# The second column group's planes split and sent one weight pair later in the up projection of a hybrid encoder layer

## The chip, the cores and the metric

The kernel runs on one core of one Trainium2 chip, as one launch. The metric is the device time of that launch in microseconds (us). The kernel before was timed three times: 1333.12, 1335.69 and 1338.51 us, median 1335.69 us.

## The reference, cut to what matters

One encoder layer on 256 tokens of width 2048, in float32: an input projection, two attention branches, a gated merge and output projection, and then an MLP of width 8192. The change lies in the MLP's first half, whose result goes on to the second half:

```python
h = rms_norm(x, norm_mlp_pre[l])
u = jnp.square(jax.nn.relu(jnp.einsum('bsd,df->bsf', h, w_up[l])))      # 256 x 8192
x = x + rms_norm(jnp.einsum('bsf,fd->bsd', u, w_down[l]), norm_mlp_post[l])
```

## The kernel before

**Numbers in two planes.** Every float32 operand of a product is split into a high plane (a cast to `F32R`, on ACT) and a low plane (the operand less the high plane, on DVE). A product is three matmuls: high by high, high by low, low by high.

**The up projection.** `w_up` (2048 x 8192) is worked off in eight groups `g` of 1024 columns, each a call of `wide_group` (L826). A group walks through eight weight pairs: pair `i` is the 256 rows from 256 `i` of the group's 1024 columns, in the order of `UPS` (L1253): 1, 2, 0, 4, 3, 6, 5, 7. Position `n` in this list is what the code counts, so n = 1 is pair 2, n = 2 pair 0, n = 3 pair 4, n = 4 pair 3. Six pairs are multiplied plainly (24 matmuls of 128x512 each); pairs 0 and 3 go by seven block products instead of eight (21 matmuls each), so a group has 186 matmuls. Results gather in eight PSUM banks; the plain pairs write banks 1, 2, 3 and 7, the seven products all but bank 7.

**One weight pair** (`pair_weights`, L696): a 1 MB load on SP's queue (L700) into one of three raw buffers; the high plane (L710, or L715 for pairs 0 and 3) on ACT into one of three buffers; the low plane (L712 or L719) on DVE into one of three. Pairs 0 and 3 also need sums of weight blocks on DVE (L716 to L718, tiles `t`), with planes of their own (`eh` on ACT, L728; `el` on DVE, L729). `Weights.next` (L750) writes the loads and splits of up to three pairs ahead into the program before the pair that is now multiplied.

**The end of a group.** After pair 3 the seven products are combined on ACT and DVE (`combine`, L820 to L824). After the last pair, 7, each of the four plain banks is added (`u_piece`, L1250, on DVE) and passed through ReLU (L1251, on ACT). The first L1250 reads bank 1, which is the bank that the next group writes first.

**What a group's result goes through during the next group** (`up_each`, L1287). A group's 1024 columns are two column groups `c` of 512. For the down projection they have to be transposed. For groups 1 to 6 this is done by DMA: `sent` (L732) splits 512 columns of both token halves into their upper and lower 16 bits (two ACT copies, L736) and issues one transposing DMA on SP's queue (L738); `joined` (L741) puts the 16-bit halves together again (one ACT copy, L743). The square follows (L1307), and `u_sets` (L1241) with `act_sets` (L1168) makes sums for the first column group (four on DVE, L1176 to L1179, tile `sm`), high planes (`ah`, L1191, ACT) and low planes (`al`, L1192, DVE), which go out to DRAM (L1195, on GpSimd's queue). The code before calls `sent` for both column groups at n = 1, `joined` for the first at n = 3 and for the second at n = 5. Group 7 transposes on TensorE.

**The down projection** reloads those planes by DMAs issued from ACT (`act_again`, L1200, L1208; tiles `bh`, `bl`).

**What sets the order.** Each engine and each DMA queue works off its instructions in the order in which they stand. That order is not the order of the Python code: the program is built with a scheduler (`schedule_with_timeline_sim`, at the top of the file) that places the instructions on each engine by its own estimate of when they can run. A call that is moved in the code thus also moves instructions that the code does not name. Temporary tiles (`page`) take their buffers from one ring of 27 in the order of the code.

## Time and profile before

| | |
|---|---|
| median of three runs | 1335.69 us |
| the profiled execution's own time | 1333.76 us |
| its span, first to last instruction | 1332.0 us |
| mean granted TensorE clock | 0.997 |
| ACT / DVE / TensorE busy | 816.1 / 1075.1 / 1319.7 us |
| up projection, groups 1 to 7 | about 687 to 988 us of the span |

Rows of a timeline give the start (us from the span's start), the duration, engine, line and operation, output and inputs by the program's names without buffer numbers, the shape, the count, and in brackets how long the engine idled before it and what released it. In the up projection three kinds of tile are called `u`: the PSUM banks, a group's result, and the transposed column groups; weight planes are `u_1h` (pair 1, high), `u_1l` (low), `u_3eh`, `u_3el`, `u_3t`, and `u_1r` is the raw load. `SPq` and `ACTq` are the DMA issues of SP and ACT. Matmuls are pipelined: one starts while the one before it is still draining.

### The profile page before, as it was taken

How to read it: one execution, taken by the hardware profiler on the slowest of the kernel's cores; microseconds unless marked ns; L12 is line 12 of the kernel's file. 1: busy time of each engine (PE TensorE's matmuls, PEld its weight loads, DVE VectorE, ACT ScalarE, POOL GpSimd, SP SyncE). 2: the span in 40 equal slices, each digit the busy share in tenths (PEclk: the TensorE clock that was granted, in tenths of full speed). 3: DMA queues.
4: the chain of work that ended last, by engine and by line, in shares of the span. 5: the costliest groups of instructions: out<-in, count | busy, mean ns of one | idle time of the engine just before them, and what ended most of it. 6: DMA issues, size and time to landing. Idle time of an engine off the chain costs nothing.

```text
span 1332.0 us, 16065 instructions
## 1 busy us (share of the span) xinstructions
PE 1319.7 (99%) x6163; PEld 1100.9 (83%) x6163; DVE 1075.1 (81%) x1245; ACT 816.1 (61%) x909; POOL 39.2 (3%) x73
## 2 busy tenths in 40 slices
PE   9999999999999999999999999999999999999997
PEld 8888888888888888888888888888888788888886
DVE  7968866777778879885678788888878888898886
ACT  6657584754554665554477788788755555555542
POOL 0000000000000000000100000000100000000000
PEclk9999999999999999999999999999999999999999
DMA  9885766665565667567658888888897998698895
GB/s 347 276 227 173 226 190 187 208 184 169 178 221 190 208 203 252 190 212 265 219 195 274 288 281 286 310 291 278 290 357 289 391 358 332 236 383 330 349 360 201
DMA packets 155917, 346.33 MB, mean 260 GB/s; under 512 B 58560, under 2 KB 59072, under 8 KB 155840
## 3 DMA queue, kind: packets, MB, share of 16 engines
q1 hardware_dynamic: 136160, 276.36, 61.6%
q10 hardware_dynamic: 12960, 43.26, 8.5%
q0 software_dynamic: 6720, 25.69, 4.7%
q8 instruction: 48, 0.79, 0.2%
q14 instruction: 29, 0.24, 0.0%
HBM read 307.01 MB, written 29.61 MB: 253 GB/s over the span
## 4 chain that ended last, share of the span: by engine, by line
PE 68%; issue 23%; DVE 4%; ACT 3%; DMA 2%; POOL 0%; SPq 0%; POOLq 0%; ACTq 0%; DVEq 0%
PE u L793 19%; PE ga L793 6%; PE gb L793 6%; PE ba L793 3%; PE bb L793 3%; PE y L793 3%; PE qn_p L224 2%; PE ka_p L224 2%; PE kn_p L224 2%; PE qa_p L224 2%; PE p L793 1%; PE qn_p L226 1%; PE ka_p L226 1%; PE vn_p L267 1%; PE vn_p L268 1%
## 5 line engine op out<-in xcount | busy, mean ns | idle before, releaser
L224 PE MATMUL qn_p<-hT,qn_h 128*128 128x512 f32 x128 | 45.5, 398 | 0.0
L793 PE MATMUL u<-u_1h,h2T 128*128 128x512 f32 x128 | 43.8, 393 | 1.5 <-DVE u L1250 1.3
L224 PE MATMUL ka_p<-hT,ka_h 128*128 128x512 f32 x128 | 45.0, 396 | 0.0
L224 PE MATMUL kn_p<-hT,kn_h 128*128 128x512 f32 x128 | 44.9, 397 | 0.0
L224 PE MATMUL qa_p<-hT,qa_h 128*128 128x512 f32 x128 | 44.2, 405 | 0.1
L793 PE MATMUL u<-u_2h,h2T 128*128 128x512 f32 x128 | 43.2, 391 | 0.0
L793 PE MATMUL u<-u_5h,h2T 128*128 128x512 f32 x128 | 41.9, 389 | 0.0
L793 PE MATMUL u<-u_6h,h2T 128*128 128x512 f32 x128 | 41.8, 389 | 0.0
L793 PE MATMUL u<-u_4h,h2T 128*128 128x512 f32 x128 | 41.5, 391 | 0.0
L793 PE MATMUL u<-u_7h,h2T 128*128 128x512 f32 x128 | 40.7, 389 | 0.0
L226 PE MATMUL qn_p<-hT,qn_l 128*128 128x256 f32 x128 | 35.9, 281 | 0.0
L226 PE MATMUL kn_p<-hT,kn_l 128*128 128x256 f32 x128 | 35.5, 280 | 0.0
L226 PE MATMUL ka_p<-hT,ka_l 128*128 128x256 f32 x128 | 34.9, 281 | 0.0
L226 PE MATMUL qa_p<-hT,qa_l 128*128 128x256 f32 x128 | 32.5, 282 | 0.1
L793 PEld LDWEIGHTS u<-u_1h,h2T 128*128 128x128 f32 x128 | 24.0, 188 | 8.3 <-ACT u L1307 3.4
L743 ACT COPY u<-u_g 128x2048 uint16<-128x2048 uint16 x12 | 30.3, 2527 | 0.0
L224 PEld LDWEIGHTS qn_p<-hT,qn_h 128*128 128x128 f32 x128 | 24.1, 188 | 5.6
L146 DVE TENSOR_TENSOR y_l<-y_w,y_h 128x1024 fp32r<-128x1024 f32 x16 | 19.0, 1222 | 11.9 <-ACT y_h L138 11.9
L712 DVE TENSOR_TENSOR u_4l<-u_4r,u_4h 128x2048 fp32r<-128x2048 f32 x8 | 18.3, 2293 | 12.5 <-ACT u_4h L710 12.5
L712 DVE TENSOR_TENSOR u_7l<-u_7r,u_7h 128x2048 fp32r<-128x2048 f32 x8 | 18.3, 2293 | 12.5 <-ACT u_7h L710 12.5
L224 PEld LDWEIGHTS kn_p<-hT,kn_h 128*128 128x128 f32 x128 | 23.8, 188 | 5.5
L224 PEld LDWEIGHTS qa_p<-hT,qa_h 128*128 128x128 f32 x128 | 24.0, 192 | 5.1 <-ACT qa_h L144 0.3
(1624 smaller groups left out, 4568.3 us busy)
## 6 DMA issues: line engine op xcount, KB each, us to landing
bh<-keeph ACTq DMA_DIRECT2D x30, 512.0 KB, 9.2
bl<-keepl ACTq DMA_DIRECT2D x30, 512.0 KB, 11.1
keeph<-ah POOLq DMA_DIRECT2D x18, 512.0 KB, 4.8
keepl<-al POOLq DMA_DIRECT2D x18, 512.0 KB, 4.7
va_w<-in_w_in SPq DMA_DIRECT2D x8, 1024.0 KB, 5.5
qn_w<-in_w_in SPq DMA_DIRECT2D x8, 1024.0 KB, 5.2
kn_w<-in_w_in SPq DMA_DIRECT2D x8, 1024.0 KB, 5.1
vn_w<-in_w_in SPq DMA_DIRECT2D x8, 1024.0 KB, 5.1
```

Source lines behind the costliest of these rows:

```text
L146: sub = nc.vector.tensor_sub(lo[part], src, hi[part].bitcast(F32)).ins
L224: nc.tensor.matmul(ps[b], hi[:, k % 4, cs], mv, start=(k == 0), stop=False)
L226: nc.tensor.matmul(ps[b][:, :T], lo[:, k % 4, cs], mv[:, :T], start=False, stop=(k == nk - 1))
L267: nc.tensor.matmul(ps[t], sh, hi[:, k % 4], start=(k == 0), stop=False)
L268: nc.tensor.matmul(ps[t], sh, lo[:, k % 4], start=False, stop=False)
L712: nc.vector.tensor_sub(l1, raw, h1.bitcast(F32))
L743: nc.scalar.copy(dst.rearrange("p k q -> p (k q)") .bitcast(U16) .rearrange("p (k t q h) -> p t h k q", k=4, t=2, h=2), got.rearrange("p ( ...
L793: ins = nc.tensor.matmul(self.ps[i], st, mv[:, blk], start=i not in self.begun, stop=last and n == 2).ins
```

## The change

One number. In `up_each` the second column group's `sent` call moves from n = 1 to n = 2, that is behind the loads and splits of pair 3 in the code; the first one's stays.

```diff
                 if by_dma and c in (0, 1):
-                    if n == (1, 1)[c]:
+                    if n == (1,2)[c]:
                         uh[cg] = sent([uz[t][:, c] for t in range(2)], f"u{cg}")
                     if n == (3,5)[c]:
                         us[cg] = page([P, 4, T], F32, f"u{cg}")
                         joined(uh[cg], us[cg])
```

What the scheduler makes of it is shown at three places of group 5; the groups 2 to 6 read alike. First ACT, in the middle of the group. `u9_s` are the split planes of the second column group of group 4 (number 9 of 16), `u8` the first one's transposed tile, `u5_3eh` the high planes of the sums of pair 3.

```order
 L710 CAST u5_6h_7380<-u5_6r_7378 128x2048
-L736 COPY u9_s_7305<-u40_7131 128x1024
-L736 COPY u9_s_7305<-u41_7132 128x1024
-L728 CAST u5_3eh0_7345<-u5_3t0_7338 128x1024
+L728 CAST u5_3eh0_7340<-u5_3t0_7333 128x1024
+L728 CAST u5_3eh1_7344<-u5_3t1_7334 128x1024
 L710 CAST u5_5h_7436<-u5_5r_7434 128x2048
-L728 CAST u5_3eh1_7349<-u5_3t1_7339 128x1024
+L736 COPY u9_s_7348<-u40_7131 128x1024
+L736 COPY u9_s_7348<-u41_7132 128x1024
+L710 CAST u5_7h_7470<-u5_7r_7468 128x2048
 L743 COPY u8_7384<-u8_g_7303 128x2x2x4x128
```

The two copies stand behind the cast of pair 5 instead of ahead of the sums' casts; the cast of pair 7 now stands ahead of the first column group's L743 instead of behind it. Further on, the cast of the next group's pair 1 stands ahead of the cast of `sm`'s planes instead of behind it. On DVE the sums of pair 3 (L716, L717) likewise stand ahead of, not behind, the low planes of pairs 3 and 6.

Second DVE, at the end of group 5 and the start of group 6. `u50` and `u51` are the result's two token halves as outputs, and as last inputs also banks of group 5; `al81` is the low plane of the column group's sums.

```order
+L712 TENSOR_TENSOR u6_1l_7512<-u6_1r_7509,u6_1h_7511 128x2048
 L1192 TENSOR_TENSOR al81_7403<-sm8_7387,ah81_7402 128x1024
-L712 TENSOR_TENSOR u6_1l_7512<-u6_1r_7509,u6_1h_7511 128x2048
 L821 TENSOR_TENSOR u50_7461<-u50_7461,u55_7371 128x512
-L712 TENSOR_TENSOR u6_2l_7542<-u6_2r_7539,u6_2h_7541 128x2048
 L822 TENSOR_TENSOR u51_7462<-u50_7461,u56_7367 128x512
 L1250 TENSOR_TENSOR u50_7461<-u50_7461,u51_7266 128x512
 L823 TENSOR_TENSOR u50_7461<-u54_7363,u50_7461 128x512
 L824 TENSOR_TENSOR u51_7462<-u54_7363,u51_7462 128x512
+L712 TENSOR_TENSOR u6_2l_7542<-u6_2r_7539,u6_2h_7541 128x2048
```

The low plane of the next group's pair 1 has moved ahead of `al81`, and that of pair 2 has moved from between L821 and L822 to behind L824, and so behind the first L1250. At the start of group 2 the order was this already in the kernel before.

Third PE, where pair 6 of group 5 ends. Before:

```order
L793 MATMUL u53_7280<-u5_6h_7380,h2T6_5190 128x512
L793 MATMUL u52_7273<-u5_5h_7436,h2T5_5189 128x512
L793 MATMUL u53_7280<-u5_5h_7436,h2T5_5189 128x512
L793 MATMUL u53_7280<-u5_5l_7437,h2T5_5189 128x512
L793 MATMUL u53_7280<-u5_5h_7436,h2T5_5189 128x512 x2
```

And now:

```order
L793 MATMUL u57_7287<-u5_6h_7380,h2T6_5190 128x512
L793 MATMUL u51_7266<-u5_5h_7436,h2T5_5189 128x512
L793 MATMUL u51_7266<-u5_5l_7437,h2T5_5189 128x512
L793 MATMUL u51_7266<-u5_5h_7436,h2T5_5189 128x512 x2
L793 MATMUL u51_7266<-u5_5l_7437,h2T5_5189 128x512
```

Before, pair 6's last matmul stood behind the first 12 of pair 5 (all of bank 51, most of bank 52); now all 24 of pair 5 stand behind it, because pair 3's matmuls moved ahead into the middle of pair 6. On SP's queue the second transposing DMA moves from behind the load of pair 5 to behind those of pair 7 and of the next group's pair 1, so the load of the next pair 2 stands directly behind it. In group 1 the order in the middle differs a little more, and at its end the cast of the next pair 2 moves behind the second column group's L743, L1307 and L1191. In group 7 and at the start of the down projection some casts and low planes change places with their neighbours; there ACT's DMA issues of the reloads (L1208) move ahead of one cast each.

## The prediction

> **What bounds the kernel now.** I read the page's busy line first, for the engine that could set the end.

> ```profile
> PE 1319.7 (99%) x6163; PEld 1100.9 (83%) x6163; DVE 1075.1 (81%) x1245; ACT 816.1 (61%) x909; POOL 39.2 (3%) x73
> ```

> TensorE is busy for 1319.7 of 1332.0 us. Next come the windows cut at two groups of the up projection (columns: length, then busy time and count of PE, PEld, DVE, ACT, POOL; granted clock, DMA share, GB/s).

> ```profile
> 815.50:858.20 42.70, 42.44 (x186) 34.83 (x187) 36.26 (x35) 34.40 (x30) 3.23 (x6) 1.00 0.89 293
> 858.20:900.80 42.60, 42.40 (x186) 34.81 (x186) 36.20 (x35) 34.56 (x30) 3.23 (x6) 1.00 0.85 288
> ```

> One group is 186 matmuls, and DVE (36.2 us) and ACT (34.5 us) have some 6 and 8 us of room in it. So a moved ACT copy costs something only if it makes TensorE wait. TensorE's own waits over the whole span are few:

> ```profile
> PE p L793 <- DMA bl<-keepl: 1.5, 1, 1.5
> PE u L793 <- DVE u L1250: 1.3, 4, 0.5
> PE u L793 <- ACT u L1307: 0.2, 1, 0.2
> ```

> The two rows of `u` are the five starts of groups 3 to 7; the first is one wait in the down projection. How much such a start really costs is read from the starts of the matmuls in the timeline of PE. Here are the first matmul of groups 2 to 7, and around the start of group 6 its neighbours.

> ```profile
> 730.07 0.39 PE L793 MATMUL u<-u_1h,h2T 128*128 128x512 f32 x1
> 772.58 0.47 PE L793 MATMUL u<-u_1h,h2T 128*128 128x512 f32 x1 [0.18 <-ACT u L1307]
> 815.51 0.47 PE L793 MATMUL u<-u_1h,h2T 128*128 128x512 f32 x1 [0.49 <-DVE u L1250]
> 858.21 0.47 PE L793 MATMUL u<-u_1h,h2T 128*128 128x512 f32 x1 [0.26 <-DVE u L1250]
> 900.22 0.39 PE L793 MATMUL u<-u_7h,h2T 128*128 128x512 f32 x1
> 900.87 0.47 PE L793 MATMUL u<-u_1h,h2T 128*128 128x512 f32 x1 [0.26 <-DVE u L1250]
> 901.18 0.40 PE L793 MATMUL u<-u_1l,h2T 128*128 128x512 f32 x1
> 902.56 0.39 PE L793 MATMUL u<-u_2l,h2T 128*128 128x512 f32 x1
> 942.90 0.39 PE L793 MATMUL u<-u_7h,h2T 128*128 128x512 f32 x1
> 943.56 0.47 PE L793 MATMUL u<-u_1h,h2T 128*128 128x512 f32 x1 [0.27 <-DVE u L1250]
> ```

> From 901.18 (second matmul of group 6) to 942.90 (its last) there are 184 steps in 41.72 us, 0.2267 us each; 186 of them are 42.17 us. The groups from 730.07 to 943.56 take 42.51, 42.93, 42.70, 42.66 and 42.69 us, so they lose 0.34, 0.76, 0.53, 0.49 and 0.52 us: **2.64 us in all**, once per group, at the start of the next. By the idle column alone the sum would be 1.5 us. [...]

> What this loss waits for is seen in the timeline of DVE at the start of group 6, where L712 makes the low planes, L821 and L822 belong to the combination, and the first L1250 frees the PSUM bank that the next group writes first.

> ```profile
> 890.96 0.43 DVE L1179 TENSOR_TENSOR sm<-u,sm 128x256 f32<-128x256 f32 x1
> 892.51 1.23 DVE L1192 TENSOR_TENSOR al<-sm,ah 128x1024 fp32r<-128x1024 f32 x1 [1.12 <-ACT ah L1191]
> 894.44 2.29 DVE L712 TENSOR_TENSOR u_1l<-u_1r,u_1h 128x2048 fp32r<-128x2048 f32 x1 [0.70 <-ACT u_1h L710]
> 896.65 0.68 DVE L821 TENSOR_TENSOR u<-u,u 128x512 f32<-128x512 f32 x1
> 897.24 2.28 DVE L712 TENSOR_TENSOR u_2l<-u_2r,u_2h 128x2048 fp32r<-128x2048 f32 x1
> 899.45 0.68 DVE L822 TENSOR_TENSOR u<-u,u 128x512 f32<-128x512 f32 x1
> 900.04 0.68 DVE L1250 TENSOR_TENSOR u<-u,u 128x512 f32<-128x512 f32 x1
> ```

> The low plane of pair 2 (2.28 us) stands between L821 and L822, so the bank is free at 900.72, and TensorE, done with its last matmul's slot at 900.45, starts at 900.87. The start of group 2 (730.07) has no such wait: there DVE ran L821 to L824 and the first L1250 before the low plane of pair 2.

> ```profile
> 726.19 0.69 DVE L1250 TENSOR_TENSOR u<-u,u 128x512 f32<-128x512 f32 x1
> 728.00 2.28 DVE L712 TENSOR_TENSOR u_2l<-u_2r,u_2h 128x2048 fp32r<-128x2048 f32 x1
> 731.66 0.39 PE L793 MATMUL u<-u_2l,h2T 128*128 128x512 f32 x1
> ```

> The bank was free at 726.88, 3.2 us early, and the low plane came at 730.28, 1.4 us before the matmul that reads it.

> **The change part by part.** No operation is added or removed: two copies (L736) and one transposing DMA per group move, in six groups (1 to 6), and by the order rows above the scheduler moves others with them. I replay group 5, from these rows of ACT, PE and SP.

> ```profile
> 874.32 1.99 ACT L736 COPY u_s<-u 128x1024 uint16<-128x1024 uint16 x2
> 877.91 1.05 ACT L728 CAST u_3eh<-u_3t 128x1024 fp32r<-128x1024 f32 x1 [1.60 <-DVE u_3t L716]
> 879.61 1.91 ACT L710 CAST u_5h<-u_5r 128x2048 fp32r<-128x2048 f32 x1 [0.64 <-PE u L793]
> 882.38 2.53 ACT L743 COPY u<-u_g 128x2048 uint16<-128x2048 uint16 x1
> 884.77 1.89 ACT L710 CAST u_7h<-u_7r 128x2048 fp32r<-128x2048 f32 x1
> 886.57 1.05 ACT L1307 ACTIVATE u<-u 128x1024 f32<-128x1024 f32 x1
> 895.21 1.92 ACT L710 CAST u_2h<-u_2r 128x2048 fp32r<-128x2048 f32 x1 [0.33 <-PE u L793]
> 892.06 0.39 PE L793 MATMUL u<-u_6h,h2T 128*128 128x512 f32 x1
> 876.34 2.01 SPq L738 DMA_TRANSPOSE u_g<-u_s  x1
> 883.88 0.37 SPq L700 DMA_DIRECT2D u_2r<-in_w_up  x1
> DMA to landing us min/median/max: 3.6/3.7/4.3
> u_2r<-in_w_up SPq DMA_DIRECT2D x8, 1024.0 KB, 6.3
> ```

> *The copies.* Their 1.99 us go from before the casts of pair 3's sums to behind the cast of pair 5. The casts had waited 1.60 us for DVE there and now run earlier, and the cast of pair 5 waits for TensorE to leave its buffer as it did, until 879.61. So the copies end at 883.5, the cast of pair 7 runs from 883.4 to 885.3 (1.4 us earlier), and the first group's copy back (L743), now behind it, ends at 887.7; its square (L1307) begins 1.1 us later than at 886.57. The four sums on DVE that need the square had been held until 7's low plane was done; they still end at about 891.3 (890.96 + 0.43 before). Cost: nothing, hidden by ACT's wait and by DVE's queue.

> *The cast of pair 1* stood behind the cast of those sums (`ah`), and now stands ahead of it. It needs the buffer of pair 6, whose last matmul began at 892.06. By the order rows of PE, pair 6's last matmul had 12 of pair 5's and pair 7's 24 behind it; now all 24 of pair 5 follow it: 48 instead of 36, so it ends 12 x 0.2267 = 2.7 us earlier, near 889.7, and ACT is free then. Cast 889.7 to 891.6, low plane to 893.9, then the sums' low part (1.2 us, its cast being done at 892.6) to 895.1.

> *The combination* follows: L821 and L822 to 896.4; the first L1250 needs the sixth of pair 7's matmuls, near 896.5, and ends at 897.2; L823 and L824 end at 898.4, and only then comes pair 2's low plane, to 900.7. Its high plane is not moved: 895.21 waits for TensorE to leave pair 5, which still has pair 7's 24 matmuls behind it. So bank 1 is free 3.2 us before 900.45, and the low plane is due at 900.45 + 7 x 0.2267 = 902.04, 1.3 us after it is ready: the same two margins as at 730.07, where no loss was seen. What is late next is that low plane.

> *The transposing DMA* waits on SP for the copies (883.5), behind the loads of pair 7 and of the next pair 1, takes 2.01 us to issue, and lands by some 3.7 us later, at 889; the copy back that reads it stands behind pair 2's cast, so not before 895.21 + 1.92 = 897.1. Queued behind it is the load of pair 2: 885.5 instead of 883.88, landing at 891.8 after 6.3 us, 3.4 us ahead of its cast. Cost: nothing.

> *Pages.* The moved copies take their two pages later, behind those of pair 3's sums. A group takes 19 pages of a ring of 27, so a page comes round after some 1.4 groups, 60 us: a shift by two places makes nobody wait.

> *Groups 1 and 7 and the down projection.* Group 1 starts group 2 without loss today and has the same order at its end, so it neither gains nor, with 1 us more on the cast of pair 2, loses. In the down projection a few casts change place with reloads of kept planes; its one wait, 1.5 us for such a reload, could go or double. I take 0 for it, as for the other reloads, none of which is among PE's waits, and keep 1.5 us to both sides.

> **Sum.** Five starts lose 2.64 us and should lose nothing: -2.6 us. The profiled execution took 1333.76 us (its span of 1332.0 and 1.8 around it), so 1331.2; against the median of 1335.69, which is 1.9 us above it, **1333.1 us**. That is 0.2%; about 0.5% (6.7 us) is what a measurement of this kernel can tell from no change.

> The largest gain is bounded by TensorE's pitch. [...]

> **The rivals.**

> *Another wait takes the place* (chance 0.17). The low plane of pair 2 gets later by 1.2 us against the matmul's start (900.7 instead of 899.5), and TensorE would arrive 0.42 us earlier. If my 1.3 us of margin is used up, the loss moves seven matmuls on and the time stays: 1335.7. For it: the margin is worked out from one group. Against it: group 2's start shows 1.4 us.

> *Slower* (chance 0.1): the copies and the copy back pile up on ACT ahead of the square, at full price 1.99 + 2.53 = 4.5 us, if the casts of pair 3's sums cannot move up. The sums on DVE then end at 895.8, their cast at 896.9, their low part at 898.1, the five vector operations from L821 to L824 (0.6 us apart, as 726.19 to 728.00 has three of them) at 901.1, and pair 2's low plane at 903.4, where 902.04 was due: 1.3 us in each of six groups, 8.0 us, less the 2.6 us won: +5.4, or 1341.1. It decides from a delay of some 3.1 us of the square on, and I work out 1.1. Against it: ACT idles 1.60 us at the very place from which the copies leave.

> *Given back in the down projection* (chance 0.08): earlier arrival meets the same reloads, and the 1.5 us wait grows to the 2.6 us won: no change, 1335.7.

> *The forecast* has 0.65: the order that it relies on already ran at one start in this trace without a loss.

> **How the numbers follow.** The range reaches down to the forecast with the down projection's wait gone (1.5 us) and the runs' own spread below their median (1335.69 - 1333.12 = 2.6 us): 1333.1 - 4.1 = 1329.0. Upward it holds no change with that wait doubled (1.5 us) and the spread above the median (1338.51 - 1335.69 = 2.8 us): 1340.0; the slower rival at its full price lies just outside, at less it lies within. No case by itself leaves the 0.5% band (1329.0 to 1342.4); only the runs' spread, added to a case at its edge, does: 0.04 faster, 0.05 slower, 0.91 within.

> **What would show it.** Right: in the waits of PE the two rows of `u` are gone; the starts of groups 2 to 7 are 42.2 us apart; on DVE the first L1250 ends some 3 us before the next group's first matmul, and pair 2's low plane after it. ACT's casts of pair 3's sums come directly behind that of pair 6. Wrong: a wait of PE for pair 2's low plane (L712) or for a cast (L710) seven matmuls into a group; starts still 42.7 us or more apart; a wait of ACT at L743 for the transposing DMA; or the wait for `bl` grown past 3 us.

## The result and the profile after

| | before | after |
|---|---|---|
| median (runs) | 1333.77 us (6, 1333.12 to 1338.51) | 1326.37 us (6, 1326.02 to 1327.03) |
| ratio, 95% interval | | 0.9939 [0.9924, 0.9953] |
| profiled execution, its span | 1333.76, 1332.0 us | 1327.03, 1325.0 us |

In a later comparison the two stood at 1332.12 us (15 runs) and 1326.02 us (5 runs): 0.9957 [0.9945, 0.9970]. The change gains some 6 to 7 us where 2.6 were forecast, and the time lies below the range.

In the waits of PE after, the rows of `u` and the row of `p` are gone. These are the longest that are left:

```profile
PE x_last L1415 <- ACT by_rows L1412: 2.2, 1, 2.2
PE idle L174 <- POOL ones L164: 1.0, 1, 1.0
PE qa_p L224 <- DVE hT L308: 0.4, 1, 0.4
```

The first matmuls of groups 2 to 7, in the timeline of PE after:

```profile
729.90 0.39 PE L793 MATMUL u<-u_1h,h2T 128*128 128x512 f32 x1
772.06 0.39 PE L793 MATMUL u<-u_1h,h2T 128*128 128x512 f32 x1
814.22 0.39 PE L793 MATMUL u<-u_1h,h2T 128*128 128x512 f32 x1
856.38 0.39 PE L793 MATMUL u<-u_1h,h2T 128*128 128x512 f32 x1
898.54 0.39 PE L793 MATMUL u<-u_1h,h2T 128*128 128x512 f32 x1
940.70 0.39 PE L793 MATMUL u<-u_1h,h2T 128*128 128x512 f32 x1
```

They are 42.16 us apart each time: the five starts lose nothing. DVE after, at the start of group 6 (898.54):

```profile
893.87 0.69 DVE L822 TENSOR_TENSOR u<-u,u 128x512 f32<-128x512 f32 x1
894.66 0.69 DVE L1250 TENSOR_TENSOR u<-u,u 128x512 f32<-128x512 f32 x1
895.27 0.68 DVE L823 TENSOR_TENSOR u<-u,u 128x512 f32<-128x512 f32 x1
895.87 0.68 DVE L824 TENSOR_TENSOR u<-u,u 128x512 f32<-128x512 f32 x1
896.47 2.28 DVE L712 TENSOR_TENSOR u_2l<-u_2r,u_2h 128x2048 fp32r<-128x2048 f32 x1
```

The bank is free at 895.35, 3.2 us early, and pair 2's low plane is ready at 898.75, 1.4 us before the eighth matmul is due (898.54 + 1.59). ACT after, in group 5:

```profile
870.51 1.91 ACT L710 CAST u_6h<-u_6r 128x2048 fp32r<-128x2048 f32 x1
872.32 1.05 ACT L728 CAST u_3eh<-u_3t 128x1024 fp32r<-128x1024 f32 x1
...
877.71 1.91 ACT L710 CAST u_5h<-u_5r 128x2048 fp32r<-128x2048 f32 x1 [0.75 <-PE u L793]
879.52 1.99 ACT L736 COPY u_s<-u 128x1024 uint16<-128x1024 uint16 x2
...
887.86 1.92 ACT L710 CAST u_1h<-u_1r 128x2048 fp32r<-128x2048 f32 x1
```

The casts of pair 3's sums stand directly behind pair 6's, the copies behind pair 5's, and pair 1's cast starts 10.7 us ahead of the next group.

**Where the 7.0 us of the spans lie**, from the starts of the matmuls: group 2 begins 0.17 us earlier; from there to the first matmul of the down projection (987.62 before, 984.68 after) 257.55 us became 254.78, **2.77 us less**; from there to the first matmul of d060 (1076.38 and 1069.59) 88.76 became 84.91, **3.85 us less**; from there to the last matmuls 0.25 us more; and behind those 6.23 became 5.77 us, 0.46 less. The second part is most of the miss. It lies in one place. The names there are those of the down projection's weight pairs: `d040` is half 0, column group 4, part 0, `d0130` is column group 13; `eh` and `el` are the planes of their sums. PE before, where the reload `bl` is waited for:

```profile
1051.97 0.39 PE L793 MATMUL p<-d031h,bl 128*128 128x512 f32 x1
1052.46 0.47 PE L793 MATMUL p<-d040h,bh 128*128 128x512 f32 x1
1052.77 0.39 PE L793 MATMUL p<-d040l,bh 128*128 128x512 f32 x1
1054.70 0.50 PE L793 MATMUL p<-d040h,bl 128*128 128x512 f32 x1 [1.54 <-DMA bl<-keepl]
1055.04 0.59 PE L793 MATMUL p<-d040h,bh 128*128 128x512 f32 x1
...
1057.56 0.63 PE L793 MATMUL p<-d040eh,bh 128*128 128x512 f32 x1
1057.99 0.63 PE L793 MATMUL p<-d040el,bh 128*128 128x512 f32 x1
...
1058.68 0.39 PE L793 MATMUL p<-d040eh,bh 128*128 128x512 f32 x1
1058.91 0.39 PE L793 MATMUL p<-d040el,bh 128*128 128x512 f32 x1
```

The matmuls behind the wait start 0.43 us apart instead of 0.2267, for 3.4 us. The windows of before say why (length; busy PE, PEld, DVE, ACT, POOL; granted clock, DMA share, GB/s):

```profile
1051.65:1055.07 3.42, 1.78 (x8) 0.87 (x7) 3.42 (x3) 1.16 (x1) 0.00 (x0) 1.00 1.03 420
1055.07:1058.48 3.41, 3.41 (x10) 2.67 (x9) 3.38 (x5) 1.53 (x3) 0.00 (x0) 0.50 1.04 422
1058.48:1061.90 3.42, 3.42 (x17) 2.81 (x16) 2.56 (x3) 1.32 (x2) 0.00 (x0) 1.00 1.01 389
```

For one stretch of 3.41 us the granted clock is 0.50: the matmuls start 0.427 us apart, so 8 of them start in it instead of 15 (3.41 / 0.2267; the counts in the windows also hold those that are still draining). In all, the 21 matmuls of d040 took 8.28 us against 4.76 (21 x 0.2267): a wait listed as 1.54 us cost 3.5 us here, and 0.26 more ahead of it. After, the same matmul waits for nothing:

```profile
1049.13 0.39 PE L793 MATMUL p<-d040h,bh 128*128 128x512 f32 x1
1049.36 0.39 PE L793 MATMUL p<-d040l,bh 128*128 128x512 f32 x1
1049.58 0.39 PE L793 MATMUL p<-d040h,bl 128*128 128x512 f32 x1
```

Two questions follow: what made the reload come in time, and what a wait costs.

### The profile page after: what moved, and what is told of

It is laid out like the page before. It is cut to its first block, busy times and chain, and to the rows that moved or that the text cites. A ratio compares the mean times of both kernels' runs of the same rounds, so it can differ in the third digit from the quotient of the medians.

```text
span 1325.0 us, 16064 instructions
## 1 busy us (share of the span) xinstructions
PE 1316.4 (99%) x6163; PEld 1100.0 (83%) x6163; DVE 1073.6 (81%) x1245; ACT 816.1 (62%) x909; POOL 39.2 (3%) x73
## 4 chain that ended last, share of the span: by engine, by line
PE 72%; issue 22%; DMA 2%; DVE 2%; ACT 1%; SPq 0%; POOL 0%; POOLq 0%; ACTq 0%
PE u L793 25%; PE ga L793 6%; PE gb L793 6%; PE ba L793 3%; PE bb L793 3%; PE y L793 3%; PE qn_p L224 2%; PE ka_p L224 2%; PE qa_p L224 2%; PE kn_p L224 2%; PE qn_p L226 1%; PE ka_p L226 1%; PE vn_p L267 1%; PE vn_p L268 1%; PE va_p L268 1%
## 5 line engine op out<-in xcount | busy, mean ns | idle before, releaser
L793 PE MATMUL u<-u_1h,h2T 128*128 128x512 f32 x128 | 43.3, 389 | 0.0
L793 PE MATMUL u<-u_2h,h2T 128*128 128x512 f32 x128 | 43.2, 391 | 0.0
L793 PE MATMUL u<-u_6h,h2T 128*128 128x512 f32 x128 | 41.9, 389 | 0.0
L793 PE MATMUL u<-u_4h,h2T 128*128 128x512 f32 x128 | 41.5, 391 | 0.0
L793 PE MATMUL u<-u_5h,h2T 128*128 128x512 f32 x128 | 41.1, 389 | 0.0
L793 PE MATMUL u<-u_7h,h2T 128*128 128x512 f32 x128 | 40.9, 389 | 0.0
L743 ACT COPY u<-u_g 128x2048 uint16<-128x2048 uint16 x12 | 30.4, 2531 | 0.0
L146 DVE TENSOR_TENSOR y_l<-y_w,y_h 128x1024 fp32r<-128x1024 f32 x16 | 19.0, 1221 | 11.9 <-ACT y_h L138 11.9
L224 PEld LDWEIGHTS kn_p<-hT,kn_h 128*128 128x128 f32 x128 | 23.8, 188 | 5.4
L712 DVE TENSOR_TENSOR u_4l<-u_4r,u_4h 128x2048 fp32r<-128x2048 f32 x8 | 18.3, 2292 | 12.2 <-ACT u_4h L710 12.2
L793 PEld LDWEIGHTS u<-u_6h,h2T 128*128 128x128 f32 x128 | 24.0, 188 | 5.0
L793 PEld LDWEIGHTS u<-u_5h,h2T 128*128 128x128 f32 x128 | 24.0, 188 | 5.0
## 6 DMA issues: line engine op xcount, KB each, us to landing
bl<-keepl ACTq DMA_DIRECT2D x30, 512.0 KB, 10.9
va_w<-in_w_in SPq DMA_DIRECT2D x8, 1024.0 KB, 6.6
qn_w<-in_w_in SPq DMA_DIRECT2D x8, 1024.0 KB, 5.1
kn_w<-in_w_in SPq DMA_DIRECT2D x8, 1024.0 KB, 5.2
vn_w<-in_w_in SPq DMA_DIRECT2D x8, 1024.0 KB, 5.3
```

What stands on the lines that cost most here:

```text
L146: sub = nc.vector.tensor_sub(lo[part], src, hi[part].bitcast(F32)).ins
L224: nc.tensor.matmul(ps[b], hi[:, k % 4, cs], mv, start=(k == 0), stop=False)
L712: nc.vector.tensor_sub(l1, raw, h1.bitcast(F32))
L743: nc.scalar.copy(dst.rearrange("p k q -> p (k q)") .bitcast(U16) .rearrange("p (k t q h) -> p t h k q", k=4, t=2, h=2), got.rearrange("p ( ...
L793: ins = nc.tensor.matmul(self.ps[i], st, mv[:, blk], start=i not in self.begun, stop=last and n == 2).ins
```

## The experiments

The runs of a row of experiments are compared with runs of the kernel before on the same chip.

**Theory 1**: two separate gains, the order on DVE at each start, and the reloads' place in ACT's queue (after, the six reload issues of column groups 4 and 5 stand ahead of the cast of d040; before, behind it, 10.2 instead of 12.9 us ahead of d040's first matmul). **Theory 2**: the reloads come in time because the up projection ends earlier.

### Groups 1 to 5 only, and group 6 only

```diff
-                    if n == (1, 1)[c]:
+                    if n == (1, 2 if g < 6 else 1)[c]:      # e1
+                    if n == (1, 2 if g == 6 else 1)[c]:     # e2
```

> The kernel before, with the second column group's copies moved one pair later in groups 1 to 5 only; group 6 stays as it was, and with it ScalarE's order in the down projection, where the six reloads of column groups 4 and 5 stand behind the cast of d040. Theory 1 (two separate gains: the place of the low plane on DVE at each group start, and the place of the reloads in ScalarE's queue): four of the five starts win their 0.34 + 0.76 + 0.53 + 0.49 = 2.1 us, the start of group 7 still loses 0.5 us, and the wait for bl with its slow matmuls stays, so about 1331.6 us against 1333.8 us, and TensorE's wait for bl is again 1 to 2 us. Theory 2 (the reloads come in time since the up projection ends earlier or since the DMA queues drain otherwise, wherever they stand in ScalarE's order): the wait for bl is gone here as well, about 1327 us.

> The kernel before, with the copies moved in group 6 only; ScalarE's order in the down projection is then that of the changed kernel, the reloads ahead of the cast of d040. Theory 1: only the start of group 7 wins (0.5 us), TensorE's wait for bl is gone and with it the matmuls at half clock (3.9 us), so about 1329.4 us against 1333.8 us. Theory 2 (the reloads need the up projection's earlier end): the wait for bl stays and the time is about 1333.2 us.

e1: 1328.96 us (1327.45 to 1332.14) against 1332.75, 0.9975 [0.9965, 0.9986]. e2: 1328.49 us (1328.20 to 1329.24), 0.9968 [0.9956, 0.9980]. In e2's profile the start of group 7 is won and no other, and TensorE waits for no reload; with four starts still lost, it stays 2.1 us above the changed kernel, as it should. So the down projection's part needs no earlier end of the up projection: Theory 2 has fallen as the whole account. e1 has the order of before there, and its runs spread over 4.7 us, e2's over 1.0. But in e1's profile TensorE did not wait for `bl` either: the order alone does not make the wait. And e1 gained 3.8 us where its four starts are worth 2.1, between what the two theories gave it; which suggests that an earlier end helps too, in part of the runs.

### The order on DVE alone

```diff
...
+            if name in ("u3_2", "u4_2", "u5_2", "u6_2", "u7_2"):
+                held.append(lambda: nc.vector.tensor_sub(l1, raw, h1.bitcast(F32)))
+                return h1, l1
...
             uw.behind = nc.vector.tensor_add(zt, zt, ps).ins
+            while held:
+                with tc.issue_after(uw.behind):
+                    held.pop()()
```

> The kernel before, copies unmoved in all groups; only pair 2's low plane of groups 3 to 7 is put behind the first L1250 of the group before it on DVE. ScalarE's order in the down projection comes out with the reloads ahead of the cast of d040. Theory 1 (the order on DVE is the whole of the group-start loss): groups 3 to 7 start without a wait, 2.6 us, and the reloads' place wins 3.9 us, so about 1327.3 us. Rival (it is the copies' place on ScalarE that matters, since pair 1's cast and low plane hold the combination back): L1250 still ends too late or the low plane comes too late for the eighth matmul, the starts win nothing, and the time is about 1329.9 us.

1333.05 us, 1.0001 [0.9993, 1.0010]: no gain. Groups 2 to 7 take 42.16, 42.27, 42.86, 42.60 and 42.40 us, 212.29 us in all: 1.2 us less than before, 1.5 more than after. The starts themselves wait for nothing now, but the loss has moved on into the group: in group 4 the first matmul that reads pair 2's low plane, due at 815.32, starts at 815.80, that plane being ready at 815.60, and some matmuls later the first of another bank waits until 817.45 (0.3 us), since the L1250 that frees this bank comes late, behind pair 2's low plane, L823 and L824. This is the prediction's rival "another wait takes the place", and it comes where the copies are not moved: the order on DVE is about half of the gain, and the other half is, as the rows suggest, that the moved copies let pair 1's cast, and with it the whole combination, come earlier. The 1.2 us were lost again in group 7, which took 45.25 us instead of 44.06 from its first matmul to that of d0130. In the down projection, whose order the edit also changed, TensorE did not wait for `bl`, but d020 lost 2.9 us.

### The reloads put back, and put back further

```diff
+        cast = nc.scalar.copy(h1[:, 1:4], raw[:, 1:4]).ins
+        if name == "d040":
+            with tc.issue_after(cast):
+                sets[0, 4], sets[0, 5] = act_again(4, 0), act_again(5, 0)
...
-                if n == 0:
+                if n == 0 and not (g == 0 and bi == 2):
```

> The changed kernel, with the six reloads of column groups 4 and 5 in the first down half put back behind the cast of d040, as they stood before; the up projection is untouched. Theory 1 (the reloads' place in ScalarE's queue): TensorE waits for bl again, 1 to 2 us, its clock falls to about half for some microseconds, and the time is about 3.9 us above the changed kernel's 1326.4 us, 1330.3 us. Theory 2 (it was the other arrival of loads, not the place): no wait, 1326.4 us.

> The changed kernel, with the six reloads of column groups 4 and 5 behind the first cast of d040's sums, some 3 us later than behind the cast of d040. Theory 1 (TensorE waits as far as the reloads' lead falls short of some 10.5 us, DMA engines being full there): the lead is 6 to 7 us, the wait for bl 3 to 4 us, a stretch at half clock follows it (1.7 us), and the time is about 1326.4 + 5 = 1331.5 us. Theory 2 (the place in the queue matters little): about 1327 us.

e8 has the same edit at the first cast of d040's sums (L728). e6: 1326.50 us (1325.85 to 1328.55); e8: 1327.29 us (1326.54 to 1332.45). Their profiled executions, 1328.55 and 1329.19 us, lie above their medians and show the wait, 1.1 and 1.8 us; the granted clock stayed at 1.00 in both. Most of the others lie within 1 us of the changed kernel's. Two of e8's ten stand at 1330.82 and 1332.45 us. So **the second half of Theory 1 has fallen too**: the reloads' own place makes the wait possible, but it is not what makes before lose in most runs.

The trace gives two times of the reload that the third matmul of d040 reads: its lead, from its issue to when that matmul was due, and its landing, from its issue to when the data were there. The issues of before, and the landings of the three `bl` among them:

```profile
1042.27 0.33 ACTq L1208 DMA_DIRECT2D bh<-keeph  x1
1042.63 0.44 ACTq L1208 DMA_DIRECT2D bl<-keepl  x1
1043.12 0.63 ACTq L1208 DMA_DIRECT2D bh<-keeph  x1
1043.78 0.48 ACTq L1208 DMA_DIRECT2D bl<-keepl  x1
```

```profile
DMA to landing us min/median/max: 7.0/10.9/14.9
```

It is the second `bl`: 1043.78 + 10.9 = 1054.68, and the matmul started at 1054.70. Its lead was 9.1 us in before, 9.0 in e6, 7.5 in e8, 9.6 in e1, 11.9 in after; its landing took 10.9, 10.2, 9.5, 9.4 and 11.5 us. After has 0.4 us to spare, before lacks 1.8. In these five, a reload with more lead mostly lands more slowly. The DMA engines are full there (a share of 1.03 to 1.04 and 420 to 422 GB/s in the first two windows above), which points to what stands ahead of it in them; that is tried below.

### The kernel before, twice more

> The kernel before, unaltered, profiled once more. Its runs spread from 1330.1 to 1338.5 us, those of the changed kernel from 1326.0 to 1327.0 us. Theory 1 (the spread is that one wait, which differs by execution since the reloads come just about in time): every step outside the down projection's column groups 2 to 5 has the same length as in the first profile, and the wait for bl another one. Rival: the spread comes from elsewhere, and the wait is 1.5 us again.

> The kernel before, unaltered, profiled a third time. Theory: the reload bl of column group 4 that the third matmul of d040 reads is issued 9.1 us ahead of that matmul again, and its landing, 10.9 us in the first profile and 9.7 us in the second, differs by execution; TensorE waits for what the landing exceeds 9.1 us by, and 3.41 us of half clock follow if a grid window holds 2.1 us of idle time or more. All other steps keep their length to 0.3 us. Rival: the landing is the same in each, and the spread of this kernel's times comes from elsewhere.

1331.25 and 1331.50 us. All steps from group 2 to d031 keep their length to 0.3 us. The landing took 9.7 and 11.0 us, and the stretch from d031's first matmul to d041's lost 1.2 and 2.6 us, against 3.8 in the first profile. The third profile's rows:

```profile
1051.35 0.47 PE L793 MATMUL p<-d040h,bh 128*128 128x512 f32 x1
1051.65 0.40 PE L793 MATMUL p<-d040l,bh 128*128 128x512 f32 x1
1053.58 0.50 PE L793 MATMUL p<-d040h,bl 128*128 128x512 f32 x1 [1.53 <-DMA bl<-keepl]
1053.91 0.39 PE L793 MATMUL p<-d040h,bh 128*128 128x512 f32 x1
```

The same wait, 1.53 us, and no half clock behind it. So the first profile showed this wait with its half clock, the dearest of the three, and the spread of the kernel before is in good part this one place.

### The reloads on SP's queue

```diff
-                nc.scalar.dma_start(t.bitcast(F32), kd)
+                (nc.sync if g == 0 and cg in (4, 5) else nc.scalar).dma_start(t.bitcast(F32), kd)
```

> The kernel before, with nothing changed but the queue of the six reloads of column groups 4 and 5 in the first half of the down projection: SP's, behind the load of d050, instead of ScalarE's. Theory 1 (lead): they are issued from about 1040.4 us on, 11.8 us ahead of the matmul that reads them instead of 10.2; the wait for bl is gone with its half clock, the five group starts still lose 2.6 us, and the time is about 1329 us, with less spread than before's. Theory 2 (the full DMA engines decide, and the load of d050 now goes ahead): the wait stays, about 1333 us.

1330.74 us against 1332.50, 0.9988 [0.9979, 0.9997]. SP issued the reload no earlier (lead 9.1 us), but it landed in 8.9 us, and the wait for `bl` is gone. The load of d041, now behind six reloads on SP, was issued 6.4 instead of 8.7 us ahead of d040's first matmul, and d021, d041, d060 and d070 lost 0.2 to 0.4 us each. So the wait can be taken away by itself, and part of what that wins is paid back.

### What makes the whole run of loads earlier

From d0130's first matmul to d040's, before (987.62 to 1052.46) and after (984.68 to 1049.13), the DMA engines moved:

```profile
DMA packets 5871, 21.62 MB, mean 334 GB/s; under 512 B 474, under 2 KB 474, under 8 KB 5867
```

```profile
DMA packets 6291, 23.10 MB, mean 358 GB/s; under 512 B 535, under 2 KB 535, under 8 KB 6287
```

After is 1.48 MB ahead, 3.5 us at 420 GB/s; e6 was at 22.98 MB, e1 at 21.80. These bytes do not sort the profiles by themselves: e6 waited 1.1 us, e1 not at all, and before's third profile, at 22.18 MB, waited 1.53 us where its second, at 21.67 MB, waited 0.53. **Theory 1b**: the order of casts sets when raw buffers come free, and so when loads start. On ACT before, then on SP:

```profile
1026.00 1.91 ACT L710 CAST d030h<-d030r 128x2048 fp32r<-128x2048 f32 x1 [2.67 <-DMA d030r<-in_w_down]
1027.81 1.04 ACT L728 CAST d020eh<-d020t 128x1024 fp32r<-128x1024 f32 x1
```

```profile
1030.27 0.37 SPq L700 DMA_DIRECT2D d031r<-in_w_down  x1
1032.00 0.37 SPq L700 DMA_DIRECT2D d040r<-in_w_down  x1
```

and the same two views of after:

```profile
1020.36 1.06 ACT L728 CAST d020eh<-d020t 128x1024 fp32r<-128x1024 f32 x1
1024.57 1.91 ACT L710 CAST d030h<-d030r 128x2048 fp32r<-128x2048 f32 x1 [3.15 <-DMA d030r<-in_w_down]
```

```profile
1024.46 0.37 SPq L700 DMA_DIRECT2D d031r<-in_w_down  x1
1028.83 0.37 SPq L700 DMA_DIRECT2D d040r<-in_w_down  x1
```

Before, the first cast of d020's sums stood behind d030's cast and waited with it for d030's load. On DVE the low plane of d030 stood ahead of the third of d020's sums, and these two are the last readers of d030's and of d020's raw buffer. DVE before, then after:

```profile
1027.94 2.29 DVE L712 TENSOR_TENSOR d030l<-d030r,d030h 128x2048 fp32r<-128x2048 f32 x1 [1.31 <-ACT d030h L710]
1031.29 0.68 DVE L718 TENSOR_TENSOR d020t<-d020t,d020r 128x512 f32<-128x512 f32 x1
```

```profile
1023.71 0.69 DVE L718 TENSOR_TENSOR d020t<-d020t,d020r 128x512 f32<-128x512 f32 x1
```

Before, the two end at 1030.23 and 1031.97, and the loads of d031 and d040 go out within 0.04 us behind them: d031's behind d030's low plane, d040's behind the third sum. After, d031's load follows the third sum (1024.40), and d040's follows d030's low plane (1028.80). So the load of d031 went out 22.2 us ahead of d040's first matmul before and 24.7 after; that of d040 hardly moved (20.5 and 20.3).

```diff
+            after = third["d020"] if name == "d030" else after           # e9: DVE only
...
+            with tc.issue_after(first["d020"]) if name == "d030" else nullcontext():
                 nc.scalar.copy(h1, raw)                                  # e10: ACT
...
```

> The kernel before with an untouched up projection; in the down projection alone, the low plane of d030 on DVE is put behind the third of d020's sums (L718), the last reader of d020's raw buffer, and the scheduler moves d021 and d040 with it: the reloads of column groups 4 and 5 then stand ahead of the cast of d040, as in the changed kernel. Theory 1b (what counts is how early the whole run of loads and reloads is issued in a stretch with full DMA engines, the reloads' own place being only a part of that): the load of d031 is issued 24 to 25 us ahead of d040's first matmul instead of 22, the DMA engines have moved 22.6 MB or more between the first matmuls of d0130 and d040 instead of 21.6 to 22.2, TensorE's wait for bl is gone, and the time falls by the 2.5 us that this wait cost on average in three profiles of the kernel before, to about 1330 us, with a narrower spread; the five starts go on losing 2.6 us. Rival (the wait went with the up projection's earlier end): about 1332.6 us and the spread as before.

> The kernel before with an untouched up projection; the high plane of d030 on ScalarE is put behind the first cast of d020's sums (L728), as it stands in the changed kernel. The scheduler then orders all of the down projection from d020 to d071 as in the changed kernel. In the run before this one the third sum (L718) alone was moved, and still waited for that cast, which stood behind the cast of d030 and so behind d030's load: the load of d031 was no earlier, and the time was unchanged. Theory 1b (the order of casts sets when raw buffers come free, so when the loads and reloads of a stretch with full DMA engines are issued): the load of d031 is issued 24 to 25 us ahead of d040's first matmul, the wait for bl is gone in nearly all executions, the starts go on losing 2.65 us, and the time is 1329.2 to 1329.8 us with a spread of about 1 us, against some 1332.5 us for the kernel before. Rival (the reloads come in time only when the up projection ends earlier): the wait and the spread stay as before, 1332.5 us.

> The changed kernel, unaltered, profiled and timed again on the same chip as the run before this one. Theory 1b: it stands 2.7 us below that one, which is the five starts, and its profile again shows no wait for bl over 0.3 us. Rival (the starts are worth more or less than their steps show, since something else gives or takes later): another difference than 2.7 us, outside 1 us on either side.

e9: 1332.71 us, 1.0000 [0.9987, 1.0013]. The edit missed its aim: on DVE the third sum came behind an L729 that still waited 2.40 us for the cast behind d030's; the load of d031 was issued 22.1 us ahead, as before, and the wait for `bl` stayed (1.8 us, half clock behind it). The miss speaks for the theory all the same: the reloads stood ahead of d040's cast there, and that helped nothing.

e10, with the up projection of before and the casts of after from d020 on: **1330.20 us** (1329.59 to 1332.27) against 1332.12, 0.9986 [0.9975, 0.9996], and a spread of 2.7 us instead of 7.8. Its load of d031 came 23.8 us ahead, and its profile has no wait for `bl`. The time stays above the 1329.2 to 1329.8 us expected; in three of eleven runs (1331.4 to 1332.3) something is left. The changed kernel on the same chip: 1326.02 us, 4.2 below e10 and not 2.7, so the rival named with this run, that something besides the starts gives too, stands. In the two profiles 2.6 us of that are the starts, 0.6 an earlier arrival at group 2, which differs among executions of one kernel by as much (729.13 to 730.07 in three of before), and the rest tenths. So on this chip the gain of 6.1 us is 1.9 for the casts' order in the down projection and 4.2 for the rest, 2.6 of them shown to be the starts. The other 1.6 are open. e2, which changes group 6 alone and has the changed kernel's order in the down projection, gained 4.3 us, 3.8 beyond its one start (0.5): twice what e10 won by the casts. e10's edit restores the lead of d031's load only in part (23.8 us; e2 24.7).

### What a wait costs

```diff
+                low_of[name] = nc.vector.tensor_sub(l1, raw, h1.bitcast(F32)).ins
...
+            low = low_of.get(f"u{g + 1}_2") if (t, half) == (0, 1) and 2 <= g < 7 else None
+            if low and g > 2:
+                with tc.issue_after(low):
+                    low = nc.vector.tensor_reduce(none[:, : g - 2],
+                        idle.unsqueeze(1).to_broadcast([P, g - 2, 512]), axis=AX.X, op=ALU.add).ins
+            with tc.issue_after(low) if low else nullcontext():
                 uw.behind = nc.vector.tensor_add(zt, zt, ps).ins
```

> The changed kernel, with the first L1250 of groups 2 to 6 put behind the next group's pair-2 low plane on DVE, and for groups 3 to 6 behind one more reduction over 512, 1024, 1536 and 2048 elements that computes nothing of use: TensorE's wait at the starts of groups 3 to 7 should be some 0.9, 1.5, 2.1, 2.6 and 3.2 us. Theory A (a wait over some bound is followed by a stretch at half clock whose cost hardly grows with it; gaps of 1.25 us without and of 1.65 and 1.70 us with one are in the runs so far): after the waits of over 1.7 us the granted clock is 0.5 for 3 to 4 us, which costs 1.7 us more each, and after the first it stays at 1.00. Theory B (the half clock has nothing to do with the wait, but with the saturated DMA engines of that stretch of the down projection): no fall at any group start. [...] Time by A about 1326.4 + 10.3 of waits + 5.1 = 1342 us, by B about 1337 us.

> The kernel with the five lengthened waits at the starts of groups 3 to 7, unaltered, profiled once more. In its first profile a wait of 2.54 us was followed by half clock and one of 2.47 us was not, so Theory A as it stood (a bound on the wait's length) has fallen. Theory A2: the granted clock is set anew on a fixed grid of 3.41 us, counted from the moment at which it first became full, and a grid window in which TensorE was idle for 2.1 us or more is followed by one window at half clock (1.7 us lost), one with 1.9 us or less is not; so far three windows of 2.16, 2.16 and 2.58 us of idle time have one behind them, and windows of 1.93, 1.78, 1.50, 1.41 and 1.37 us have none. The grid begins elsewhere in every execution, so the same waits should fall differently here, but each by that rule. Rival B2: the half clock comes with the place in the program; then again only the start of group 6 has one.

> The same kernel and the same two theories a third time: by A2 each of the five waits is followed by a window of half clock if, and only if, 2.1 us or more of it lie in one window of the grid; by B2 the start of group 6 alone.

The edit is made on the changed kernel. 1338.95 us, where the kernel before took 1332.50 on this chip, 1.0051 [1.0035, 1.0066]; the repeats 1339.14 and 1338.79. By the steps, the starts idled 0.3, 1.7, 1.4, 2.7 and 2.5 us. In the first profile half clock came behind the fourth alone: the fifth, nearly as long, had none. That ended Theory A (a bound on the wait's length). Around the fifth, first profile, in windows of 3.4133 us (measured below), counted from the moment at which the clock first became full:

```profile
947.13:950.54 3.41, 2.15 (x10) 1.46 (x8) 3.41 (x2) 3.35 (x4) 0.00 (x0) 1.00 0.92 334
950.54:953.95 3.41, 2.35 (x10) 1.99 (x11) 3.41 (x6) 3.41 (x5) 0.53 (x1) 1.00 1.02 394
```

and in the second, where the same wait fell into one window:

```profile
949.26:952.67 3.41, 1.15 (x5) 1.01 (x6) 3.41 (x5) 3.39 (x4) 0.53 (x1) 1.00 1.01 363
952.67:956.08 3.41, 3.41 (x10) 2.65 (x9) 3.41 (x4) 2.11 (x4) 0.53 (x1) 0.50 0.83 324
```

The grid is read off the traces: the half clock of before lasts 3.413 us, and the clock is full ahead of it from 7.17 to 1055.07, for 1047.89 us, which is 307 windows of 3.4133 us; after has full clock from 5.35 to 1319.48, 385.0 of them; in these two runs the falls come 264.0, 263.0 and 277.0 windows after their first. TensorE's idle time within a window (steps between starts less 0.2267 for each matmul) then sorts all windows at full clock that have more than 1.35 us of it, up to the end of the down projection (values that are alike stand once):

| idle in one window, us | granted clock in the next |
|---|---|
| 2.78, 2.58, 2.34, 2.27, 2.18, 2.16 (before), 2.16 | 0.50 for 3.41 us |
| 1.93, 1.81 (before, third), 1.78, 1.77, 1.50, 1.41, 1.40, 1.37 | 1.00 |

The rows are from the three runs here and from before, before's third profile, e4, e6, e8 and e9. Rule A2 of the repeats held in both, and the rival (the place in the program) fell with the first of them, where half clock also came behind the fifth start. A window at half clock lost 1.5 to 1.6 us by these steps.

## Why the prediction was wrong

- **The five starts**: right. 2.64 us were to go, 2.69 went between the first matmuls of groups 2 and 7 (213.49 us became 210.80); 3.2 and 1.4 us of margin where 3.2 and 1.3 were worked out; the moves of the casts, of the copies and of pair 1's cast came as replayed, and the copies cost nothing.
- **What was late next** in a group: nothing; the two rivals that a start or a group would lose did not come.
- **The down projection**: wrong, and this is the step that failed. "In the down projection a few casts change place with reloads of kept planes; its one wait, 1.5 us for such a reload, could go or double. I take 0 for it ... and keep 1.5 us to both sides." The wait went, and it was worth more than its row. Two things were left out. The order rows showed casts change place, and I did not follow them as I did in the up projection: a cast that waits for a load, put ahead of other work, holds back the release of the raw buffers that later loads need (here d031's load went out 22.2 instead of 24.7 us ahead), and in a stretch with full DMA engines (420 GB/s) this has a share in whether the reloads are in time (1.9 us by e10). And a wait's price was taken as the idle column's 1.54 us, where the steps of the matmuls behind it, in the same trace, showed 3.5 (over three profiles of before, the stretch from d031 to d041 lost 3.8, 1.2 and 2.6 us).
- **The rival "given back in the down projection"** had the sign of this place wrong: with the new order of casts an earlier arrival met earlier loads.
- **The base**: 1333.1 - 1326.4 = 6.7 us of miss are 4.8 in the size of the change (7.4 against 2.6) and 1.9 in the median: that of the first three runs, 1335.69 us, was high. The range took the spread of these runs for noise of the measurement; in good part it was the wait itself, which the change takes away, and so its lower end stood too high.
- **Open**: the 0.46 us behind the last matmul. It is 6.2 to 6.3 us in five profiles (three of before, e4, e5) and 5.5 to 5.9 in the others, with no edit there. Why e6 mostly loses nothing at the lead of before is argued from the bytes moved, and not shown by itself. Of the down projection's part, e10 shows 1.9 us to come from the order of casts; e2 won twice that, and what makes the difference was not taken apart.

## What to carry to other kernels

Where a trace of before has a wait that the change's reordering touches, price it by the steps of the instructions behind it and not by the idle column (3.5 against 1.54 us in before's first profile), and follow its loads back to the buffers and casts that release them. A kernel whose runs spread by 5 us (before: 1333.12 to 1338.51) may, as this one, have one transfer that lands just about in time (before lacked 1.8 us, after had 0.4 to spare); profile it twice before its spread is taken for noise. Moving the code of one stage can reorder the next, and the larger part may lie there (here 3.85 of 7.0 us).

## What was unexpected of the hardware

The same 512 KB reload took 8.9 us (e5) to 13.1 us (e9) to land, with some 420 GB/s moving in all around the wait (before, 1051.65 to 1058.48); issued 2.8 us earlier against its need (after, 11.9 instead of 9.1) it landed only 2.2 us earlier against it.
